# Contiguous operands for the gate-matrix matmuls of a hybrid decoder layer

## The chip, the cores and the metric

The kernel runs on one core of a Trainium2 chip. The metric is the device time of one execution in microseconds (us). Engines are TensorE (PE in the profile; PEld its weight loads), VectorE (DVE), ScalarE (ACT), GpSimd (POOL) and SyncE (SP). SP, ACT and POOL also issue DMAs.

## What is computed

One layer: RMSNorm, an input projection, differential attention and an mLSTM in parallel, an output projection, then PEER, a retrieval of single-neuron experts, and a gated embedding at the end. The change is in PEER. For each of 1024 tokens and 8 heads it finds 16 experts among 128 x 128 by two half keys, with softmax weights:

```python
eidx = jnp.take_along_axis(cidx, pos, axis=-1)      # i0 * 128 + i1
g = jax.nn.softmax(top_s, axis=-1)
a = jax.nn.gelu(jnp.einsum('td,thkd->thk', xb, expert_u[eidx]), approximate=False)
return jnp.einsum('thk,thkd->td', (g * a), expert_v[eidx])
```

## The kernel before

**Stages.** `front(0)` and `front(1)` do norms, projections, attention, mLSTM and the top-k of half the tokens each. `dense_up`, `dense_down` and `tail` follow. Three of the eight token tiles (NS = 3) take the experts by gathers (`sparse`: 384 gathers `ru` from expert_u, each multiplied on VectorE in line 808, and 384 `rv` from expert_v, accumulated into `ya` in line 826). The other five tiles (NDT = 5, 640 tokens, TD) are done densely: all 16384 experts are computed and weighted by a gate matrix that is zero where an expert was not chosen.

**The up stage** (`dense_up`) loops over 128 columns j. Each loads a table of 128 experts (`raw`, 512 KB, on SP's queue, three tiles), ScalarE rounds it to `thi` (line 845, two tiles), VectorE makes the rest `tlo` (line 846), and TensorE forms A: 24 matmuls of 384 token columns and 24 of 256, in the order (thi with the rounded and the rest of the tokens, then tlo). ScalarE applies GELU out of PSUM into `ga` (line 958, two pieces) and its queue stores it to `ga_s`. At each j, `pump` also lets 0.9 (the first 40 columns) or 1.45 pairs of gathers of `sparse` be emitted, at a lower priority than everything near (LAG = 800).

**The gate blocks** (`gate_blocks`) build the gate matrix, token by token: for a token t, the 128 x 128 matrix of gates is the product of two one-hot matrices over its 128 (head, k) pairs, the second weighted. The 128 pairs lie on the partitions. `it` holds, per partition, i0, i1, the weight rounded to 16 bits, and the rest of the weight, each for 128 tokens. Groups of 16 tokens are handled together: 40 groups in all. VectorE writes `o0` (i0 equals iota), `o1` (i1 equals iota), `w0` = o1 x weight and `w1` = o1 x rest, each 2048 fp16 elements laid out as [4, 128, 4]: the token b = 0 to 3 is innermost, so neighbours in memory are four tokens and `o0[:, a, :, b]`, the operand of one token, has a step of four elements. For each quarter a, eight matmuls (four tokens, w0 and w1, lines 898 and 899) fill one PSUM tile `pg` (three tiles), and ScalarE copies it to `st` (line 901; 512 elements, written with a step of GB = 32 elements). Each of o0, o1, w0 and w1 is one tile. After two groups `st` (32 tokens, 2 MB) is stored to `g_s` on SP's queue (line 904).

**Order.** The order on each engine is fixed when the program is built: a scheduler takes the instructions by their place in the program text and by when its model says that they are ready. Gate groups are emitted only after `late`, the top-k of the remaining tiles, is used up. From then on, after column j, the loop of line 965 emits groups until done x GSP >= (j - GST) x nb, with GSP = 105, GST = 14, and nb = 40 `yield`s of the generator. When `late` ends, the groups that are due by then come together. The sequence on VectorE that gathers and `tlo` share is held together by `anchor` and `behind`.

**The down stage** (`dense_down`) reads `g_s` and `ga_s` back, multiplies them, and accumulates with expert_v; `tail` ends the layer.

Of the kernel before, what the change touches and what calls it, by code (L numbers as in the profile page):

```python
# [11 lines left out]
F16 = mybir.dt.float16  # L12
I32 = mybir.dt.int32
U32 = mybir.dt.uint32
AF = mybir.ActivationFunctionType
OP = mybir.AluOpType
# [3 lines left out]
P = 128  # L20
# [19 lines left out]
NDT = S // P - NS  # L40
# [16 lines left out]
LATE = 1  # L57
HEAD = 200
WIDE = ("r1", "ro", "ry", "r2")
ACTW = 0  # L60
VB = 1
KORD = ("h", "r", "l")
GSP = 105
# [3 lines left out]
GB = 32  # L67
# [10 lines left out]
def layer(ctx, tc, x, xT, pT, gcols, grows, win, convw, convb, gbias, lams, wout, wq, subk,  # L78
# [3 lines left out]
    def pool(name, bufs=1, **k):  # L82
        if k.get("space") != bass.MemoryType.DRAM:
            k["reuse_waits"] = "tile"
        return tc.tile_pool(name=name, bufs=bufs, **k)

    v, sc, pe, gp, sy = nc.vector, nc.scalar, nc.tensor, nc.gpsimd, nc.sync
# [5 lines left out]
    def load_const(src, shape, name, pl_=const, dt=F32):  # L93
        t = pl_.tile(shape, dt, name=name)
        sy.dma_start(t, src)
        return t
# [752 lines left out]
    def table(dp, src, raw=None):  # L849
        raw = dp.tile([P, 1024], F32, name="raw", bufs=3) if raw is None else raw  # L850
        hi = dp.tile([P, 1024], F32R, name="thi", bufs=2)
        lo = dp.tile([P, 1024], F32R, name="tlo", bufs=2)
        split(raw, src, hi, lo)
        return hi, lo

    def gate_blocks(gp_, pT_, pG):
        ioe = gp_.tile([P, P, 4], F16, name="ioe")
        iof = load_const(iota_d[None, :].to_broadcast([P, P]), [P, P], "iof", gp_)
        v.tensor_copy(ioe, iof[:, :, None].to_broadcast([P, P, 4]))
        sh = [P, 4, P, 4]  # L860
        io = ioe[:, None].to_broadcast(sh)
        for n, tl in enumerate(DORD):
            part, i = divmod(tl, NT)
            fl = gp_.tile([P, 3, P], F32, name="fl", bufs=1)
            v.tensor_copy(fl[:, 0], sel_i[part][0][:, i, :])
            v.tensor_copy(fl[:, 1], sel_i[part][1][:, i, :])
            v.tensor_scalar(fl[:, 2], gsm[part][:, i, :], WSC, None, op0=OP.mult)
            pt = pT_.tile([P, 3, P], F32, name="pt")
            for c in range(3):
                pe.transpose(pt[:, c, :], fl[:, c, :], ident)  # L870
            it = gp_.tile([P, 4, P], F16, name="it", bufs=2)
            v.tensor_copy(it[:, 0:3], pt)
            v.tensor_tensor(it[:, 3], pt[:, 2], it[:, 2], op=OP.subtract)
            if ACTW:
                wlo = fl[:, 2]
                v.tensor_tensor(wlo, pt[:, 2], it[:, 2], op=OP.subtract)
            for hb in range(P // GB):
                st = gp_.tile([P, P, GB], F32, name="st", bufs=64 // GB)
                for sb in range(GB // 16):
                    tb = slice(hb * GB + sb * 16, hb * GB + sb * 16 + 16)  # L880
                    iv = [it[:, c, tb].rearrange("p (a b) -> p a b", b=4)[:, :, None, :].to_broadcast(sh)
                          for c in range(4)]
                    o0 = gp_.tile(sh, F16, name="o0", bufs=1)
                    o1 = gp_.tile(sh, F16, name="o1", bufs=1)
                    w0 = gp_.tile(sh, F16, name="w0", bufs=1)
                    w1 = gp_.tile(sh, F16, name="w1", bufs=1)
                    v.tensor_tensor(o0, iv[0], io, op=OP.is_equal)
                    v.tensor_tensor(o1, iv[1], io, op=OP.is_equal)
                    v.tensor_tensor(w0, o1, iv[2], op=OP.mult)
                    if ACTW < 4:  # L890
                        v.tensor_tensor(w1[:, :4 - ACTW], o1[:, :4 - ACTW], iv[3][:, :4 - ACTW], op=OP.mult)
                    for a in range(4):
                        for b in range(4) if a >= 4 - ACTW else ():
                            t_ = hb * GB + sb * 16 + a * 4 + b
                            sc.activation(w1[:, a, :, b], o1[:, a, :, b], AF.Copy, scale=wlo[:, t_:t_ + 1])
                        pg = pG.tile([P, 4, P], F32, name="pg")
                        for b in range(4):
                            pe.matmul(pg[:, b, :], o0[:, a, :, b], w0[:, a, :, b], start=True, stop=False)  # L898
                            pe.matmul(pg[:, b, :], o0[:, a, :, b], w1[:, a, :, b], start=False, stop=True)  # L899
                        t_ = sb * 16 + a * 4  # L900
                        sc.activation(st[:, :, t_:t_ + 4].rearrange("p j t -> p t j"), pg, AF.Copy,
                                      scale=1.0 / WSC)
                    yield True
                sy.dma_start(g_s[n * (P // GB) + hb], st)

    def chain(*gens):
        for g in gens:
            yield from g()

    def dense_up(ptk):  # L910
        qh, ql = fcs["q"]
        chunks = [(qh, ql, 0, CH1)]
        with ExitStack() as c1:
            dp = c1.enter_context(pool("dp"))
            gp_ = c1.enter_context(pool("gp"))
            pA = c1.enter_context(pool("pA", bufs=2, space=PSUM))
            pT_ = c1.enter_context(pool("pT_", space=PSUM))
            pG = c1.enter_context(pool("pG", bufs=3, space=PSUM))
            raw = dp.tile([P, 1024], F32, name="raw", bufs=3)
            gas = [dp.tile([P, TD], F32, name="ga", bufs=3)]  # L920
            if NX:
                xh = dp.tile([P, DC, NX], F32R, name="xh")
                xl = dp.tile([P, DC, NX], F32R, name="xl")
                chunks.append((xh, xl, CH1, TD - CH1))

            head = [table(dp, ut[0], raw)]

            def extra_columns():
                for n, tl in enumerate(DORD[CH1 // P:]):
                    h2 = gp_.tile([P, D], F32, name="st", bufs=64 // GB)  # L930
                    sy.dma_start(h2, h2_s[tl])
                    for q in range(2):
                        pt = pT_.tile([P, 4, P], F32, name="pt")
                        for j in range(4):
                            pe.transpose(pt[:, j, :], h2[:, (4 * q + j) * P:(4 * q + j + 1) * P], ident)
                        dst = (slice(None), slice(4 * q, 4 * q + 4), slice(n * P, (n + 1) * P))
                        sc.activation(xh[dst], pt, AF.Copy)  # L937
                        v.tensor_sub(xl[dst], pt, xh[dst].bitcast(F32))

            late = chain(lambda: topk2(0, ptk, [2]), lambda: topk2(1, ptk, [0, 2]))  # L940
            gates = gate_blocks(gp_, pT_, pG)
            nb, done = 8 * NDT, 0
            for j in range(P):
                pump(UP_RATE[0 if j < UP_RATE[2] else 1])
                hi, lo = head.pop() if head else table(dp, ut[j])
                ga = gas.pop() if gas else dp.tile([P, TD], F32, name="ga", bufs=3)
                ps = pA.tile([P, 2, 512], F32, name="A")
                terms = [[(ps[:, n, :w], hi[:, dc * P:(dc + 1) * P], lo[:, dc * P:(dc + 1) * P], rh[:, dc, :w],
                           rl[:, dc, :w], dc == 0, dc == DC - 1) for dc in range(DC)]
                         for n, (rh, rl, o, w) in enumerate(chunks)]  # L950
                if j == 0:
                    mm3s(terms[0], ("hr", "l"))
                    extra_columns()
                    mm3s(sum(terms[1:], []), ("hr", "l"))
                else:
                    mm3s(sum(terms, []), ("hr", "l"))
                for n, (rh, rl, o, w) in enumerate(chunks):
                    sc.activation(ga[:, o:o + w], ps[:, n, :w], AF.Gelu)
                sc.dma_start(ga_s[j], ga)
                if late is not None:  # L960
                    for _ in range(LATE):
                        if late is not None and next(late, None) is None:
                            late = None
                    continue
                while done < nb and done * GSP < (j - GST) * nb:
                    next(gates, None)
                    done += 1
            for _ in gates:
                pass
# [292 lines left out]
```

## Time and profile before

| | us |
|---|---|
| median of 3 runs (3181.86 to 3189.38) | 3186.96 |
| profiled execution | 3192.56 |
| span of its instructions | 3190.8 |
| TensorE busy in the span | 2954.2 (93%) |
| VectorE busy | 2512.5 (79%) |
| ScalarE busy | 1159.0 (36%) |
| the up stage, first A matmul to last `ga` | 1031 to 2115 |
| gate matmuls, first to last | 1362 to 2044 |

A row of a group of instructions reads: line, engine, operation, output and inputs, shape, count, then busy us and mean ns of one, then the idle time of the engine before them and what ended it. A matmul's record begins when it starts streaming and ends when its result is out, so matmuls overlap: how far apart two start tells what one costs in a stream.

### The profile page before, as it was taken

How to read it: one execution, taken by the hardware profiler on the slowest of the kernel's cores; microseconds unless marked ns; L12 is line 12 of the kernel's file. 1: busy time of each engine (PE TensorE's matmuls, PEld its weight loads, DVE VectorE, ACT ScalarE, POOL GpSimd, SP SyncE). 2: the span in 40 equal slices, each digit the busy share in tenths (PEclk: the TensorE clock that was granted, in tenths of full speed). 3: DMA queues.
4: the chain of work that ended last, by engine and by line, in shares of the span. 5: the costliest groups of instructions: out<-in, count | busy, mean ns of one | idle time of the engine just before them, and what ended most of it. 6: DMA issues, size and time to landing. Idle time of an engine off the chain costs nothing.

```text
span 3190.8 us, 44623 instructions
## 1 busy us (share of the span) xinstructions
PE 2954.2 (93%) x16367; PEld 2599.5 (81%) x16367; DVE 2512.5 (79%) x5321; ACT 1159.0 (36%) x1992; POOL 1021.9 (32%) x786
## 2 busy tenths in 40 slices
PE   7997889887777999999899999988999999999987
PEld 6786767776666899999899999977878888887866
DVE  5564689887679998777877768667888888888886
ACT  5664335555322222264333343322212222222233
POOL 0000000343312433403554435443434444342331
PEclk9998989998798999999999999989999999999998
DMA  5333433676745877858998989999999999998773
GB/s 165 96 106 110 144 119 96 211 230 203 255 178 178 311 276 264 302 217 308 344 355 333 335 300 342 345 368 337 333 334 339 338 338 333 332 317 277 265 236 126
DMA packets 317147, 829.52 MB, mean 260 GB/s; under 512 B 26240, under 2 KB 115200, under 8 KB 314368
## 3 DMA queue, kind: packets, MB, share of 16 engines
q0 software_dynamic: 112608, 410.04, 36.3%
q1 hardware_dynamic: 185888, 374.68, 33.9%
q10 hardware_dynamic: 18432, 41.95, 3.5%
q8 instruction: 128, 2.10, 0.3%
q14 instruction: 91, 0.75, 0.1%
HBM read 715.95 MB, written 102.24 MB: 256 GB/s over the span
## 4 chain that ended last, share of the span: by engine, by line
PE 29%; DMA 7%; DVE 7%; issue 7%; POOL 1%; ACT 1%; DVEq 0%; SPq 0%; POOLq 0%; ACTq 0%
PE A L145 13%; PE keep L145 6%; DMA raw<-in_vr 3%; DMA rv<-in_ev,eidx 2%; PE Y L137 2%; PE Y L136 2%; PE Y L138 2%; DVE ya L826 2%; PE pg L898 1%; PE pg L899 1%; DMA ru<-in_eu,eidx 1%; DVE tlo L846 1%; DVE ru L808 1%; DVE aq L1024 1%; DVE yac L1045 1%
## 5 line engine op out<-in xcount | busy, mean ns | idle before, releaser
L792 POOL DMA_INDIRECT ru<-in_eu,eidx x384 | 499.5, 1301 | 1165.4 <-DVE ru L808 857.0
L792 POOL DMA_INDIRECT rv<-in_ev,eidx x384 | 514.4, 1340 | 465.7 <-DVE ya L826 321.1
L826 DVE SCALAR_TENSOR_TENSOR ya<-rv,cf,ya 128x1024 f32<-128x1024 f32 x384 | 492.5, 1283 | 44.6 <-DMA rv<-in_ev,eidx 33.6
L846 DVE TENSOR_TENSOR tlo<-raw,thi 128x1024 fp32r<-128x1024 f32 x256 | 312.5, 1221 | 263.5 <-ACT thi L845 143.6
L845 ACT ACTIVATE thi<-raw 128x1024 fp32r<-128x1024 f32 x256 | 267.8, 1057 | 685.4 <-PE A L145 353.5
L808 DVE SCALAR_TENSOR_TENSOR ru<-ru,sh 128x1024 f32<-128x1024 f32 x384 | 467.9, 1219 | 27.0 <-DMA ru<-in_eu,eidx 24.4
L145 PE MATMUL A<-ahi,thi 128*128 128x384 f32 x1024 | 349.5, 341 | 14.1 <-ACT thi L845 13.8
L145 PE MATMUL A<-alo,thi 128*128 128x384 f32 x1024 | 346.9, 339 | 0.2 <-issue 0.2
L145 PE MATMUL mm<-ahi,whi 128*128 128x512 f32 (+1 forms) x752 | 300.0, 403 | 21.2 <-ACT ahi L236 12.8
L145 PE MATMUL mm<-alo,whi 128*128 128x512 f32 (+1 forms) x752 | 286.6, 394 | 7.1 <-DVE alo L237 7.1
L136 PE MATMUL Y<-thi,ph 128*128 128x512 f32 x640 | 250.8, 392 | 7.5 <-ACT thi L845 5.6
L137 PE MATMUL Y<-tlo,ph 128*128 128x512 f32 x640 | 250.1, 391 | 2.1 <-DVE tlo L846 2.1
L145 PE MATMUL A<-xh,thi 128*128 128x256 f32 x1024 | 251.3, 283 | 0.7 <-ACT xh L937 0.7
L145 PE MATMUL A<-xl,thi 128*128 128x256 f32 x1024 | 251.3, 283 | 0.0
L138 PE MATMUL Y<-thi,pl 128*128 128x512 f32 x640 | 249.3, 390 | 0.0
L1025 ACT ACTIVATE ph<-aq 128x640 fp32r<-128x640 f32 x128 | 87.4, 728 | 338.1 <-PE Y L137 332.9
L145 PEld LDWEIGHTS A<-ahi,thi 128*128 128x128 f32 x1024 | 195.5, 191 | 14.4 <-ACT thi L845 14.0
L145 PE MATMUL A<-ahi,tlo 128*128 128x384 f32 x1024 | 201.1, 336 | 0.3 <-DVE tlo L846 0.3
L145 PE MATMUL mm<-ahi,wlo 128*128 128x512 f32 (+1 forms) x752 | 193.1, 388 | 5.5 <-DVE wlo L196 5.5
L145 PEld LDWEIGHTS A<-xh,thi 128*128 128x128 f32 x1024 | 195.4, 191 | 0.9 <-ACT xh L937 0.9
L145 PEld LDWEIGHTS A<-alo,thi 128*128 128x128 f32 x1024 | 195.3, 191 | 0.5 <-issue 0.5
L145 PEld LDWEIGHTS A<-xl,thi 128*128 128x128 f32 x1024 | 195.4, 191 | 0.0
(462 smaller groups left out, 6121.4 us busy)
## 6 DMA issues: line engine op xcount, KB each, us to landing
raw<-in_ut SPq DMA_DIRECT2D x128, 512.0 KB
raw<-in_vr SPq DMA_DIRECT2D x128, 512.0 KB
ga_s<-ga ACTq DMA_DIRECT2D x128, 320.0 KB
g_s<-st SPq DMA_DIRECT2D x20, 2048.0 KB
gq<-g_s SPq DMA_DIRECT2D x32, 1280.0 KB
aq<-ga_s SPq DMA_DIRECT2D x32, 1280.0 KB
wraw<-in_win SPq DMA_DIRECT2D x58, 512.0 KB
wraw<-in_wq SPq DMA_DIRECT2D x32, 512.0 KB
```

Source lines behind the costliest of these rows:

```text
L136: pe.matmul(o, lh, rh, start=start, stop=False)
L137: pe.matmul(o, lh, rl, start=False, stop=False)
L138: pe.matmul(o, ll, rh, start=False, stop=stop)
L145: pe.matmul(o, ll if p == "l" else lh, rl if p == "r" else rh, start=start and p == "h", stop=stop and n == last and p == names[-1])
L792: gp.indirect_dma_start(out=b, out_offset=None, in_=table, in_offset=bass.IndirectOffsetOnAxis(ap=eidx[part][:, i, k:k + 1], axis=0))
L808: behind(v.scalar_tensor_tensor(b, b, 1.0, st["h", tl], op0=OP.mult, op1=OP.mult, accum_out=st["d", n][:, j:j + 1]))
L826: op = v.scalar_tensor_tensor(ya, b, st["c", n][:, j:j + 1], ya, op0=OP.mult, op1=OP.add)
L845: sc.activation(hi, raw, AF.Copy)
L846: anchor(v.tensor_sub(lo, raw, hi.bitcast(F32)))
L898: pe.matmul(pg[:, b, :], o0[:, a, :, b], w0[:, a, :, b], start=True, stop=False)
L899: pe.matmul(pg[:, b, :], o0[:, a, :, b], w1[:, a, :, b], start=False, stop=True)
L1025: sc.activation(ph, av, AF.Copy)
```

## The change

`o0` is now laid out [16, 128], each token's 128 elements contiguous, and written by one compare whose first input repeats each token's i0 over 128 places and whose second is the iota (every fourth element of the tile `ioe`, which holds each number four times). `o1` and `w0` keep the interleaved layout; `o1` is overwritten in place by o1 x rest, and `w1` is gone. For each half group (a = 0 and a = 2) ScalarE copies the two weighted matrices, eight tokens each, from the interleaved order into a new tile `wc`, one tile in size of w1, contiguous for each token: two copies of 1024 elements. The matmuls read `o0` and `wc`. The compare for o0 moves behind the other three VectorE operations. The generator yields after each half group, and nb is 80 in place of 40. The setting ACTW, which was 0, and the code under it are removed.

```diff
-                    o0 = gp_.tile(sh, F16, name="o0", bufs=1)
+                    o0 = gp_.tile([P, 16, P], F16, name="o0", bufs=1)
                     o1 = gp_.tile(sh, F16, name="o1", bufs=1)
                     w0 = gp_.tile(sh, F16, name="w0", bufs=1)
-                    w1 = gp_.tile(sh, F16, name="w1", bufs=1)
-                    v.tensor_tensor(o0, iv[0], io, op=OP.is_equal)
                     v.tensor_tensor(o1, iv[1], io, op=OP.is_equal)
                     v.tensor_tensor(w0, o1, iv[2], op=OP.mult)
-                    if ACTW < 4:
-                        v.tensor_tensor(w1[:, :4 - ACTW], o1[:, :4 - ACTW], iv[3][:, :4 - ACTW], op=OP.mult)
+                    v.tensor_tensor(o1, o1, iv[3], op=OP.mult)
+                    v.tensor_tensor(o0, it[:, 0, tb][:, :, None].to_broadcast([P, 16, P]),
+                                    ioe[:, None, :, 0].to_broadcast([P, 16, P]), op=OP.is_equal)
                     for a in range(4):
+                        if a % 2 == 0:
+                            wc = gp_.tile([P, 2, 2, 4, P], F16, name="wc", bufs=1)
+                            for c, w in enumerate((w0, o1)):
+                                sc.activation(wc[:, c], w[:, a:a + 2].rearrange("p a j b -> p a b j"), AF.Copy)
                         pg = pG.tile([P, 4, P], F32, name="pg")
                         for b in range(4):
-                            pe.matmul(pg[:, b, :], o0[:, a, :, b], w0[:, a, :, b], start=True, stop=False)
-                            pe.matmul(pg[:, b, :], o0[:, a, :, b], w1[:, a, :, b], start=False, stop=True)
+                            for c in range(2):
+                                pe.matmul(pg[:, b, :], o0[:, 4 * a + b, :], wc[:, c, a % 2, b, :], start=c == 0,
+                                          stop=c == 1)
...
-                    yield True
+                        if a % 2:
+                            yield True
...
-            nb, done = 8 * NDT, 0
+            nb, done = 16 * NDT, 0
```

## Rows read from the trace of the kernel before

**Rows 1.** The span in 40 slices: busy tenths of TensorE and of DMA
```profile
PE   7997889887777999999899999988999999999987
...
DMA  5333433676745877858998989999999999998773
```

**Rows 2.** Windows: length, busy us of PE, PEld, DVE, ACT, POOL, clock, DMA, GB/s
```profile
1100.00:1200.00 100.00, 100.00 (x684) 100.00 (x683) 98.22 (x311) 29.87 (x47) 41.92 (x32) 1.00 0.79 290
1356.00:1500.00 144.00, 143.99 (x1078) 138.62 (x1077) 118.22 (x122) 83.55 (x100) 29.19 (x21) 1.00 0.67 246
1500.00:2116.00 616.00, 602.68 (x4249) 598.56 (x4247) 461.34 (x519) 228.35 (x320) 303.80 (x224) 0.99 0.91 339
1356.00:2116.00 760.00, 746.67 (x5325) 737.17 (x5323) 579.56 (x641) 311.90 (x419) 332.99 (x245) 0.99 0.87 321
2116.00:3035.00 919.00, 886.10 (x3844) 725.84 (x3844) 761.19 (x972) 221.00 (x275) 357.56 (x273) 0.98 0.93 325
```

**Rows 3.** Windows of the gate tile pg alone: length, PE, ACT, clock, DMA, GB/s
```profile
1356.00:1500.00 144.00, 65.87 (x512) 63.66 (x64) 1.00 0.67 246
```

**Rows 4.** Groups of 16-bit matmuls and weight loads; L415 loads by minimum/median/maximum ns
```profile
L898 PE MATMUL pg<-w,o 128*128 128x128 f16 x640 | 152.5, 297 | 11.4 <-DVE w L889 11.4
...
L899 PEld LDWEIGHTS <-o 128*128 128x128 f16 x640 | 75.1, 117 | 3.8 <-issue 2.6
...
L415 PE MATMUL S<-maskneg,identb 128*128 128x128 bf16 x64 | 14.8, 232 | 0.0
...
L415 PEld LDWEIGHTS <-identb x64: 95/96/152, 53.3 to 784.8; 128*128 128x128 bf16 x64
```

**Rows 5.** Timeline of single matmuls: start us, duration us, engine, line
```profile
1409.55 0.29 PE L899 MATMUL pg<-w,o 128*128 128x128 f16 x1
...
1410.13 0.30 PE L898 MATMUL pg<-w,o 128*128 128x128 f16 x1
...
1414.19 0.28 PE L145 MATMUL A<-xh,thi 128*128 128x256 f32 x1
...
1415.02 0.28 PE L145 MATMUL A<-xl,thi 128*128 128x256 f32 x1
...
1413.15 0.33 PE L145 MATMUL A<-ahi,thi 128*128 128x384 f32 x1
...
1414.02 0.33 PE L145 MATMUL A<-alo,thi 128*128 128x384 f32 x1
...
699.84 0.39 PE L145 MATMUL mm<-alo,whi 128*128 128x512 f32 x1
...
701.44 0.39 PE L145 MATMUL mm<-ahi,whi 128*128 128x512 f32 x1
```

**Rows 6.** Groups of VectorE, shapes kept apart
```profile
L887 DVE TENSOR_TENSOR o<-it,ioe 128x2048 f16<-128x2048 f16 x40 | 49.0, 1224 | 51.7 <-PE pg L899 51.7
...
L846 DVE TENSOR_TENSOR tlo<-raw,thi 128x1024 fp32r<-128x1024 f32 x256 | 312.5, 1221 | 263.5 <-ACT thi L845 143.6 <-issue 117.5
...
L1141 DVE TENSOR_TENSOR yac<-gt,yac 128x512 f32<-128x512 f32 x10 | 6.6, 682 | 0.0
...
L749 DVE COPY i<-dl 128x256 bf16<-128x256 bf16 x4 | 1.1, 278 | 0.0
...
L751 DVE COPY bb<-pos 128x256 bf16<-128x256 bf16 x4 | 0.9, 218 | 0.0
```

**Rows 7.** Groups of ScalarE between 1031 and 2116 us
```profile
L901 ACT ACTIVATE st<-pg 128x512 f32<-128x512 f32 x160 | 159.5, 1141 | 37.5 <-PE pg L899 35.5 <-issue 1.9
L845 ACT ACTIVATE thi<-raw 128x1024 fp32r<-128x1024 f32 x128 | 135.8, 1061 | 429.1 <-PE A L145 353.5 <-DVE ya L826 39.3 <-remote 10.3
L958 ACT ACTIVATE ga<-A 128x384 f32<-128x384 f32 (+1 forms) x256 | 98.4, 437 | 171.1 <-PE A L145 152.0 <-issue 19.0
...
L937 ACT ACTIVATE xh<-pt 128x512 fp32r<-128x512 f32 x4 | 2.4, 598 | 13.0 <-PE pt L935 13.0
```

**Rows 8.** Waits from 1356 to 2046 us: total us, times, longest us
```profile
ACT thi L845 <- PE A L145: 199.9, 60, 4.7
...
DVE o L887 <- PE pg L899: 51.7, 34, 2.4
...
PE pg L898 <- DVE w L889: 11.4, 1, 11.4
```

More of the change, by code (lines that the diff above doesn't have):

```diff
@@ L59 @@
 WIDE = ("r1", "ro", "ry", "r2")
-ACTW = 0
 VB = 1
@@ L873, in gate_blocks @@
             v.tensor_tensor(it[:, 3], pt[:, 2], it[:, 2], op=OP.subtract)
-            if ACTW:
-                wlo = fl[:, 2]
-                v.tensor_tensor(wlo, pt[:, 2], it[:, 2], op=OP.subtract)
             for hb in range(P // GB):
@@ L882, in gate_blocks @@
                           for c in range(4)]
-                    o0 = gp_.tile(sh, F16, name="o0", bufs=1)
+                    o0 = gp_.tile([P, 16, P], F16, name="o0", bufs=1)
                     o1 = gp_.tile(sh, F16, name="o1", bufs=1)
                     w0 = gp_.tile(sh, F16, name="w0", bufs=1)
-                    w1 = gp_.tile(sh, F16, name="w1", bufs=1)
-                    v.tensor_tensor(o0, iv[0], io, op=OP.is_equal)
                     v.tensor_tensor(o1, iv[1], io, op=OP.is_equal)
                     v.tensor_tensor(w0, o1, iv[2], op=OP.mult)
-                    if ACTW < 4:
-                        v.tensor_tensor(w1[:, :4 - ACTW], o1[:, :4 - ACTW], iv[3][:, :4 - ACTW], op=OP.mult)
+                    v.tensor_tensor(o1, o1, iv[3], op=OP.mult)
+                    v.tensor_tensor(o0, it[:, 0, tb][:, :, None].to_broadcast([P, 16, P]),
+                                    ioe[:, None, :, 0].to_broadcast([P, 16, P]), op=OP.is_equal)
                     for a in range(4):
-                        for b in range(4) if a >= 4 - ACTW else ():
-                            t_ = hb * GB + sb * 16 + a * 4 + b
-                            sc.activation(w1[:, a, :, b], o1[:, a, :, b], AF.Copy, scale=wlo[:, t_:t_ + 1])
+                        if a % 2 == 0:
+                            wc = gp_.tile([P, 2, 2, 4, P], F16, name="wc", bufs=1)
+                            for c, w in enumerate((w0, o1)):
+                                sc.activation(wc[:, c], w[:, a:a + 2].rearrange("p a j b -> p a b j"), AF.Copy)
                         pg = pG.tile([P, 4, P], F32, name="pg")
                         for b in range(4):
-                            pe.matmul(pg[:, b, :], o0[:, a, :, b], w0[:, a, :, b], start=True, stop=False)
-                            pe.matmul(pg[:, b, :], o0[:, a, :, b], w1[:, a, :, b], start=False, stop=True)
+                            for c in range(2):
+                                pe.matmul(pg[:, b, :], o0[:, 4 * a + b, :], wc[:, c, a % 2, b, :], start=c == 0,
+                                          stop=c == 1)
                         t_ = sb * 16 + a * 4
```

## Prediction

> **What bounds the kernel now.** I read the page's slices first, then the windows of the stage that the change touches, then its groups of instructions, then single matmuls in the timeline. The slices [rows 1] show TensorE nearly full from the first third of the span to the end, with the DMA engines nearly full too from the middle on. The gate blocks run inside the up stage, between 1356 and 2116 us. There TensorE is busy 746.67 of 760 us, VectorE 579.56, ScalarE 311.90, at clock 0.99 [rows 2]: TensorE sets the end of this stage. The stage falls in two. In the first 144 us, 512 of the 1280 gate matmuls run, 16 of the 40 groups of 16 tokens, and DMA is at 0.67; in the other 616 us the gates are thin and DMA stands at 0.91 with 339 GB/s [rows 2, 3]. Waits of TensorE for the gates' operands are one of 11.4 us in the whole stage [rows 8]. So what the change takes from TensorE is gained, unless something else fills the 760 us: DMA moves 321 GB/s over them [rows 2], 244 MB, and is the next in line.
>
> **What a gate matmul costs.** It has 128 columns and yet one starts every 116 ns: 0.58 us for five steps from 1409.55 to 1410.13 [rows 5]. Matmuls with contiguous operands start every 119 ns at 256 columns (0.83 us for seven), 174 ns at 384 (0.87 for five) and 229 ns at 512 (1.60 for seven) [rows 5]. That is about 55 ns for 128 columns, and a line through them gives 64 ns at 128. The gate matmul thus pays for 256 columns. Its record says the same: 297 ns, while the one matmul of this kernel with 16-bit contiguous operands of 128 columns lasts 232 ns, 65 ns less; and its weight load lasts 117 ns against 96 [rows 4]. What sets the gates apart is that both operands are read with a step of four elements, 8 bytes. I take 64 ns after the change. The ends are 55 ns (only the slope) and 117 ns (the step is not the cause). In between lies 96 ns, if the contiguous weight load of that length paces the pair.
>
> [...]
>
> **The change part by part.** TensorE: 1280 x (117 - 64) ns = 68 us less (ends 79 and 0, at 96 ns 27 us). The stage would last 692 us if TensorE went on setting it.
>
> VectorE: the first operand is still one compare of 2048 elements, but its inputs are now a value repeated with step 0 and an iota read with step 4, and no longer four neighbours at a time. Now it takes 1224 ns, as long as 1024 fp32 elements (1221): two 16-bit elements where fp32 has one [rows 6]. Where a 16-bit copy in this trace reads a repeated value, 256 elements cost 278 ns instead of 218 [rows 6], so packing does suffer. I take one element at a time: 512 fp32 elements cost 682 ns, 1024 cost 1221, 1.053 ns each, so 2048 cost 1221 + 1078 = 2299 ns. 40 x 1.08 = 43 us more, and nothing at the low end; below nothing is excluded, since the pattern loses neighbours and wins none. The multiplication that wrote w1 now writes o1 and costs what it did. VectorE goes to 623 us, 87% of the 714 us forecast below. Earlier in the stage it was busy 98.22 of 100 us with TensorE full [rows 2], so I cost this at nothing; if the cover is gone it is 43 us.
>
> ScalarE: per 16 tokens four copies are added, each of 1024 16-bit elements, read with step 4, written contiguous; 160 in all. No row shows a 16-bit source read so. The nearest is the copy of 1024 fp32 elements, 1061 ns. The low end is half of that, 0.53 us, if 16-bit goes two at a time. The high end comes from the copy out of PSUM that writes with a step of 32 elements: 1141 ns for 512, where a contiguous one takes 598 [rows 7], 1.06 ns more per element, so 1.06 + 1.09 = 2.15 us. I take 1.06, since the new copy writes contiguous and reads with a short step: 160 x 1.06 = 170 us (85 to 344). ScalarE goes from 312 to 482 us of the stage. Nothing on the path, if it is spread: it waits 199.9 us for A matmuls to free the thi tile [rows 8].
>
> The new waits: a copy waits for w0 and o1, and, wc being one tile, for the 16 matmuls that read the last one. Behind a waiting copy on ScalarE stand thi (the next column's table), the GELU ga and its DMA on the same queue, and the copies out of PSUM. TensorE waits for thi, VectorE for thi before tlo, and tlo stands before the sparse part's gathers. In return VectorE no longer waits for the gate matmuls before it rewrites w0 and o1, only for the copies; o0 alone still waits for TensorE (these waits cost VectorE 51.7 us [rows 8]). After the first 144 us a half group comes every 1.3 columns (80 over the 105 of GSP), over 9 us at 24 x (119 + 174) ns = 7.0 us of A matmuls per column, and its two copies take 2.1: hidden. In the first 144 us, 16 groups come at once. On ScalarE one costs 4 x 1.06 + 4 x 1.14 = 8.8 us, where now a group passes every 9 us (144/16): the gates then proceed at ScalarE's pace, and TensorE fills with A matmuls of later columns, which need from ScalarE only 1.06 us for thi and 2 x 0.44 for ga [rows 7] per 7 us. I cost it at nothing; what it costs without that cover is the last rival's price. That the generator hands over half groups, twice as often, changes only where in the order they stand. SBUF is the same: w1 leaves, wc of equal size comes. The store of st to g_s stays in SP's queue ahead of raw loads of later columns; it waits for the last copy out of PSUM as now, and three raw tiles are ahead of need: no cost while the groups do not fall behind.
>
> DMA: no byte changes, but the same 244 MB come in less time. The first part shortens by 512 x 53 ns = 27 us to 117. The other 339 GB/s x 616 us = 209 MB would take 560 us at full share (339/0.91 = 373 GB/s), and then TensorE's 692 us for the stage hold; with no more throughput than now they take 616, the stage 117 + 616 = 733. These are 68 and 27 us of gain. I take the middle, 350 GB/s or 0.94: 597 + 117 = 714 us, a gain of 46. The down stage runs at 0.93 [rows 2], so a share like that holds for long, but with TensorE full only in part (886 of 919 us). The stages behind start when A ends and nothing of theirs changes, so the gain reaches the end.
>
> **Sum.** The profiled execution took 3192.56 us, its span 3190.8. 3192.6 - 46 = 3147. The median of the runs before is 5.6 us under that execution: 3141 us.
>
> **Rivals.** DMA doesn't bind: gathers move into the first 144 us, where DMA has a third free, and TensorE keeps its 68 us: 3119 us. For it, the low share at the beginning; against it, VectorE does those gathers and is fullest there.
>
> The weight load paces the pair at 96 ns: 27 us, 3160. For it, loads and matmuls alternate one to one; against it, a gate load lasts as long as its slot, which would be so for either operand.
>
> The operands' step is not the cause, or the change doesn't reach it: nothing saved, VectorE's and ScalarE's additions hidden, 3187. [...] For it, the 256-column matmul has the same 117 ns; against it the two record lengths.
>
> ScalarE sets the pace where 16 groups come at once, and the A matmuls do not fill in, since thi stands behind gate copies in ScalarE's order. A group then lasts 8.8 us plus half a column's thi and ga (1.0), 9.8, where TensorE needs 32 x 64 ns and half a column of A, 3.5 us, together 5.5. 16 x 4.3 = 69 us lost eats the whole 68. Above 1.06 us per copy the kernel is slower: at 1.5 us a group lasts 11.5 and 16 x 6.0 = 96 us are lost, 28 net: 3215. For it, ScalarE's fixed order and the one wc tile; against it, in the trace ScalarE's waits are for TensorE, not the reverse.
>
> **Chances.** Forecast (3119 to 3160) 0.52, no bound by DMA 0.13, load-paced 0.10, nothing saved 0.09, ScalarE's pace 0.16. A measurement of this kernel tells about 0.2%, 6.4 us, from no change. Faster: 0.52 + 0.13 + 0.10 = 0.75. Nothing saved is mostly the same, 0.07, with 0.02 to slower: 0.18. The range takes in the 55 ns end (79 us, 3108) and goes up to 3184, where the pair would save next to nothing; it leaves out ScalarE's pace and little else.
>
> **What would show it.** In the profile after: gate matmuls 64 ns apart and near 232 ns long, with loads near 96; the o0 compare at 2.3 us; 160 copies at 1.06; TensorE as full as before from 1356 on and DMA at 0.94 behind the burst; A's last matmul 46 us earlier and the down stage as long as now. It is wrong if gate matmuls stay at 117 ns, if copies pass 1.5 us, or if TensorE shows new waits for wc or thi.

## The result and the profile after

The changed kernel takes 3140.26 us (median of four runs, 3135.79 to 3143.68) beside 3185.61 (3181.86 to 3189.38; four runs, one more than in the table above) before: a ratio of 0.9854 [0.9836, 0.9872], its 95% interval in brackets, 45 us less. 3141 was forecast. The profiled execution took 3138.16 us, its span 3136.4, so the two profiles lie 54.4 us apart; that of before was 7 us above its median, that of after 2 under.

The slices of the page after, busy tenths, as in [rows 1]:

```profile
PE   7997889987789799999999999979999999999987
...
ACT  5664326554422232257787656422222222222133
...
DMA  5333423566664788889998999999999999998763
```

TensorE is nearly as full as before, with one dip to 7 where the up stage ends; ScalarE has its new work from the eighteenth slice on. Where the 54.4 us lie is read from the first and the last A matmul (count, minimum/median/maximum ns, first and last start). First two rows of before, then two of after:

```profile
L145 PE MATMUL A<-ahi,thi x1024: 334/334/687, 1031.4 to 2109.6; 128*128 128x384 f32 x171
L145 PE MATMUL A<-xh,tlo x1024: 275/281/560, 1050.4 to 2114.1; 128*128 128x256 f32 x171
```

```profile
L144 PE MATMUL A<-ahi,thi x1024: 331/335/690, 1039.1 to 2056.9; 128*128 128x384 f32 x171
L144 PE MATMUL A<-xh,tlo x1024: 277/282/365, 1058.1 to 2061.3; 128*128 128x256 f32 x171
```

From first to last A matmul it is 2114.1 - 1031.4 = 1082.7 us before and 2061.3 - 1039.1 = 1022.2 after: 60.5 us less. The stage began 7.7 us later, with the order of the instructions up to there unchanged (over all kernels of this study it began between 1028 and 1039). The down stage took 911.3 in place of 914.7 us, the tail 158.0 in place of 156.4. 60.5 - 7.7 + 3.4 - 1.6 = 54.6. The whole gain thus lies in the up stage, and I compare the kernels below by these 1082.7 and 1022.2 us beside their times. Such a length comes from one execution and is not exact: two kernels below, whose gate matmuls and whose times are as before, have 1074.1 and 1074.2 us.

The windows of the stage after, columns as in [rows 2], and one of pg alone, columns as in [rows 3]:

```profile
1365.00:1500.00 135.00, 126.23 (x1027) 121.05 (x1026) 125.58 (x128) 107.81 (x126) 62.76 (x43) 1.00 0.89 325
1500.00:1710.00 210.00, 196.72 (x1594) 188.29 (x1594) 195.74 (x196) 166.49 (x195) 95.80 (x69) 1.00 0.91 340
1710.00:2005.00 295.00, 293.75 (x2276) 291.69 (x2276) 253.57 (x265) 184.54 (x232) 151.98 (x111) 1.00 0.95 357
1365.00:2062.00 697.00, 673.32 (x5281) 657.45 (x5279) 613.30 (x632) 471.68 (x575) 339.59 (x244) 1.00 0.93 347
```

```profile
1364.00:1708.00 344.00, 62.63 (x816) 106.76 (x102) 1.00 0.90 334
```

The gates that come together now take 344 us, not 144: 816 of the 1280 gate matmuls, 25.5 groups, one every 13.5 us. TensorE idles in that part (135.00 - 126.23 and 210.00 - 196.72, 22 us) and hardly behind it (1.25 us of 295). VectorE is at 93% there (125.58 of 135, 195.74 of 210), ScalarE at 80% and 79%.

The groups of the gates between 1031 and 2070 us (busy us, mean ns of one, idle before them by what ended it), which answer to [rows 4], [rows 6] and [rows 7]:

```profile
L895 PE MATMUL pg<-wc,o 128*128 128x128 f16 x1280 | 94.4, 220 | 23.3 <-ACT wc L891 21.1 <-ACT st L898 0.9 <-issue 0.7
L895 PEld LDWEIGHTS <-o 128*128 128x128 f16 x1280 | 75.7, 98 | 38.9 <-issue 33.1 <-DVE o L885 0.3 <-PE A L144 0.2
L891 ACT ACTIVATE wc<-w 128x1024 f16<-128x1024 f16 x80 | 92.1, 1151 | 18.8 <-DVE w L883 17.6 <-ACT ga L956 1.2
L891 ACT ACTIVATE wc<-o 128x1024 f16<-128x1024 f16 x80 | 91.7, 1146 | 13.2 <-DVE o L884 11.5 <-ACT ga L956 1.6
L885 DVE TENSOR_TENSOR o<-it,ioe 128x2048 f16<-128x2048 f16 x40 | 91.5, 2288 | 3.2 <-PE pg L895 2.6 <-PE A L144 0.2
```

And the waits between 1364 and 2062 us (who waits, for whom: sum, count, longest), as in [rows 8]:

```profile
ACT thi L844 <- PE A L144: 93.9, 54, 4.6
...
DVE o L882 <- ACT wc L891: 22.2, 23, 2.1
PE pg L895 <- ACT wc L891: 21.1, 24, 1.0
ACT wc L891 <- DVE w L883: 17.6, 21, 1.6
DVE o L885 <- PE pg L895: 2.6, 6, 1.0
...
DVE ya L825 <- DMA rv<-in_ev,eidx: 1.8, 2, 0.9
DVE ru L807 <- DMA ru<-in_eu,eidx: 1.3, 3, 0.8
```

The matmul's record has gone from 297 to 220 ns, its weight load from 117 to 98. VectorE's 51.7 us of waits for gate matmuls have become 2.6, and 22.2 for the copies. New is a row of TensorE: 24 waits for `wc`, up to 1.0 us each, 21.1 us in all. One of them in the timeline, first of TensorE and then of ScalarE (start, duration, line; in brackets the idle time before it):

```profile
1450.52 0.34 PE L144 MATMUL A<-ahi,thi 128*128 128x384 f32 x1
1451.82 0.27 PE L895 MATMUL pg<-wc,o 128*128 128x128 f16 x2 [0.96 <-ACT wc L891]
...
1452.86 0.96 PE L895 MATMUL pg<-wc,o 128*128 128x128 f16 x14
1453.63 0.42 PE L144 MATMUL A<-ahi,thi 128*128 128x384 f32 x1
```

```profile
1450.63 1.14 ACT L891 ACTIVATE wc<-w 128x1024 f16<-128x1024 f16 x1
1451.64 1.14 ACT L891 ACTIVATE wc<-o 128x1024 f16<-128x1024 f16 x1
```

The first copy ends at 1450.63 + 1.14 = 1451.77 us; TensorE, which had A matmuls to do, stands from 1450.86 to 1451.82. The gates' place in its order comes before those A matmuls. The 14 matmuls behind the second copy show the new price: (0.96 - 0.22)/13 = 57 ns apart.

Two figures are worked out from the start times of all matmuls in the stage. Neighbouring gate matmuls start 118 ns apart before and 56 after (medians): 1280 x 62 = 79 us less. And where a gate matmul follows an A matmul, the time between their starts beyond the usual 174 or 119 ns sums to 12.0 us before (11.6 of them in one step, the wait of 11.4 in [rows 8]) and to 30.7 after, over 50 steps: 19 us more. I call this second sum the excess. 79 - 19 = 60, the measured 60.5. The clock has no part in the 118 and 56 ns: the granted clock is 1.00 in the burst before [rows 2] and in the one after, and an A matmul of 384 columns takes 174 ns in both. The sum holds for this pair of executions; between kernels with the same matmuls the length differs by 8 us, as said above. So the question for the experiments is what makes TensorE wait in front of the gates, and which operand's order was worth the 79 us.

### The profile page after: what moved, and what is told of

Same layout as the page of the kernel before. It is cut to its first block, busy times and chain, and to the rows that moved or that the text cites. A ratio compares the mean times of both kernels' runs of the same rounds, so it can differ in the third digit from the quotient of the medians.

```text
span 3136.4 us, 44806 instructions
## 1 busy us (share of the span) xinstructions
PE 2890.3 (92%) x16367; PEld 2531.0 (81%) x16367; DVE 2552.5 (81%) x5321; ACT 1320.9 (42%) x2152; POOL 1027.0 (33%) x786
## 4 chain that ended last, share of the span: by engine, by line
PE 62%; DVE 12%; issue 10%; DMA 9%; ACT 5%; POOL 2%; SPq 0%; DVEq 0%; ACTq 0%; POOLq 0%
PE A L144 24%; PE mm L144 11%; PE keep L144 7%; DMA raw<-in_vr 3%; PE Y L136 3%; PE Y L135 3%; PE Y L137 3%; DMA rv<-in_ev,eidx 3%; PE S L144 2%; PE pg L895 2%; DVE ya L825 2%; DVE ru L807 1%; ACT st L898 1%; DMA ru<-in_eu,eidx 1%; ACT wc L891 1%
## 5 line engine op out<-in xcount | busy, mean ns | idle before, releaser
L807 DVE SCALAR_TENSOR_TENSOR ru<-ru,sh 128x1024 f32<-128x1024 f32 x384 | 468.0, 1219 | 23.7 <-DMA ru<-in_eu,eidx 23.7
```

What stands on the lines that cost most here:

```text
L807: behind(v.scalar_tensor_tensor(b, b, 1.0, st["h", tl], op0=OP.mult, op1=OP.mult, accum_out=st["d", n][:, j:j + 1]))
```

## The experiments

Three theories of the 19 us: **S**, the single tile `wc` ties copies and matmuls to each other; **D**, DMA, which the prediction named: TensorE is held back because tables or gathers come late; **O**, the order fixed in advance puts gate matmuls close behind copies that end later than was allowed for. Each ratio below is to runs of the kernel before on the same chip, whose medians were 3191.55 to 3192.64 us there, so ratios and not times compare with the 0.9854 above.

**A second tile wc.** `it` and `ga` give up a buffer and the iota moves into the place of `fl`, so that it fits.

```diff
-wc = gp_.tile([P, 2, 2, 4, P], F16, name="wc", bufs=1)
+wc = gp_.tile([P, 2, 2, 4, P], F16, name="wc", bufs=2)
```

> The changed kernel (3140 us) with two wc tiles instead of one; to make room in SBUF, ga has two tiles instead of three, it one instead of two, and the iota is loaded into the place of fl. Theory S (TensorE's gain is partly given back because the copies of a half group wait for the matmuls that read the one wc tile, and TensorE then waits for the copies): the 24 waits of about 1 us for wc in the changed kernel's up stage (21 us) mostly go, and the time falls by 10 to 24 us, to 3116 to 3130. Theory D (DMA takes it back): the stage stays as long, 3134 to 3146.

3141.74 us, ratio 0.9841 [0.9824, 0.9858]; first to last A matmul 1030.2 us. Two rows of its waits in the stage:

```profile
PEld L896 <- DVE o L886: 16.4, 3, 10.4
...
PE pg L896 <- ACT wc L892: 13.9, 7, 12.4
```

The many waits of about 1 us for `wc` are gone (7 in place of 24), but one of 12.4 us came, and one of 10.4 for VectorE's o0. The time that S forecast did not come back: the kernel is no faster. This alone does not refute S, since `ga` and `it` have fewer buffers here and the order is another one; the run doesn't say what a second tile would bring in the same order.

**Gates spread over the stage.** They start later and follow at a steady pace.

```diff
-GSP = 105
-GST = 14
+GSP = 75
+GST = 44
```

> The changed kernel with its gate groups spread: GST = 44 and GSP = 75, so that no groups are overdue when the gates begin, one half group per column. Theory S: where groups come one at a time, ScalarE keeps up, TensorE's waits for wc (21 us) vanish, 3116 to 3130. Theory D: the DMA load per time is the same in the mean, 3134 to 3146.

3135.37 us, 0.982 [0.9799, 0.984]; 1028.3 us from first to last A matmul. The row of TensorE's waits:

```profile
PE pg L895 <- ACT wc L891: 26.9, 26, 4.7
```

The waits stay, and the excess is 35.0 us. The time is in D's range, and its interval overlaps that of the changed kernel run again (0.9844 [0.9821, 0.9867], below), so a gain is not shown. That 26 groups come back to back is thus not by itself their cause.

**Half the bytes of the tables.** Each column loads 512 of its 1024 values per partition and reads them twice; the other half of each table is left out.

```diff
-raw = dp.tile([P, 1024], F32, name="raw", bufs=3)
+raw = dp.tile([P, 512], F32, name="raw", bufs=3)
+sy.dma_start(raw, src[:, 0:512])
+rb = raw[:, None, :].to_broadcast([P, 2, 512])
```

> The changed kernel with half the table loaded in the up stage: each column's raw holds 512 of its 1024 elements per partition, and ScalarE and VectorE read them twice (so the dense part computes with wrong tables; the work of every engine is the same). 33.6 MB fewer, about a tenth of what DMA moves in the stage. Theory D: with the DMA engines relieved the stage ends 20 us or more earlier, 3120 or below. Theory S: nothing waits for DMA there, 3134 to 3146.

3137.69 us, 0.9842 [0.9819, 0.9864]; 1021.0 us from first to last A matmul. Its window of the stage and its row of waits:

```profile
1360.00:2055.00 695.00, 671.49 (x5272) 656.14 (x5271) 610.91 (x629) 470.67 (x573) 339.25 (x244) 1.00 0.87 318
```

```profile
PE pg L899 <- ACT wc L895: 23.1, 27, 1.0
```

DMA has fallen from 0.93 and 347 GB/s to 0.87 and 318, and neither the time nor the waits have moved. D falls: the stage isn't held by DMA.

**Only the moving operand contiguous.** o0 goes back to the interleaved layout and its old compare; the copies into `wc` stay.

```diff
-o0 = gp_.tile([P, 16, P], F16, name="o0", bufs=1)
+o0 = gp_.tile(sh, F16, name="o0", bufs=1)
-pe.matmul(pg[:, b, :], o0[:, 4 * a + b, :], wc[:, c, a % 2, b, :], start=c == 0,
+pe.matmul(pg[:, b, :], o0[:, a, :, b], wc[:, c, a % 2, b, :], start=c == 0,
```

> The changed kernel with o0 interleaved as before (and its compare as before); only the moving operand wc is contiguous. Theory: the moving operand's step of 8 bytes is what cost the second half of each gate matmul's 117 ns, so the matmuls start 56 to 64 ns apart here too; the weight loads stay at 117 ns each by their records, beside the matmuls. Rival (the weight load with that step sets the pace): about 117 ns apart, time 3186. If it is shared, something between, such as 96 ns.

A single execution: 3133.52 us beside 3191.88 of the kernel before. Its groups:

```profile
L894 PE MATMUL pg<-wc,o 128*128 128x128 f16 x1280 | 95.6, 221 | 26.2 <-ACT wc L890 25.7
L894 PEld LDWEIGHTS <-o 128*128 128x128 f16 x1280 | 80.6, 115 | 41.2 <-issue 32.9 <-DVE o L885 2.4 <-DVE tlo L845 0.3
```

The matmuls start 56 ns apart and last 221 ns, as with both contiguous, though the loads are back at 115 ns.

**Only the stationary operand contiguous.** o0 as in the change; w1 is back and the matmuls read the interleaved w0 and w1; no copies.

```diff
+w1 = gp_.tile(sh, F16, name="w1", bufs=1)
-v.tensor_tensor(o1, o1, iv[3], op=OP.mult)
+v.tensor_tensor(w1, o1, iv[3], op=OP.mult)
-wc[:, c, a % 2, b, :]
+(w0, w1)[c][:, a, :, b]
```

> The changed kernel with o0 contiguous, but the moving operands w0 and w1 interleaved as before and read directly, so without the copies on ScalarE. Theory (the moving operand's step is the cause): the gate matmuls start 117 ns apart, time 3180 to 3192. Rival (the weight load's step is): 56 to 64 ns apart, and as nothing waits for copies the time is at or below that of the changed kernel, 3105 to 3140.

3191.37 us beside 3191.55, 1.0007 [0.9993, 1.0021]. Its groups:

```profile
L892 PE MATMUL pg<-w,o 128*128 128x128 f16 x1280 | 158.8, 294 | 10.7 <-DVE w L884 6.8 <-DVE o L886 3.9
L892 PEld LDWEIGHTS <-o 128*128 128x128 f16 x1280 | 139.8, 114 | 16.2 <-DVE w L884 7.4 <-DVE o L886 4.4 <-issue 1.4
```

116 ns apart, records of 294, 1074.2 us from first to last A matmul: nothing is gained. The two runs together show that all of the 79 us comes from the moving operand. The load lasts 114 ns here though its operand is contiguous (98 in the changed kernel, whose matmuls start 56 ns apart), so its record also follows the pace of the matmuls. This kernel also has the 2.3 us compare, and no loss: its 43 us on VectorE are hidden here, beside slow matmuls.

**A contiguous iota** for the o0 compare, of which the value repeated with step 0 stays.

```diff
+ioc = gp_.tile([P, P], F16, name="ioc")
+v.tensor_copy(ioc, iof)
-ioe[:, None, :, 0].to_broadcast([P, 16, P])
+ioc[:, None, :].to_broadcast([P, 16, P])
```

> The changed kernel with the second input of the o0 compare contiguous (an iota of its own in fp16) while the first still repeats one value with step 0. If the repeated value keeps the compare at one element at a time, it stays at 2.29 us; if the iota's step of four did, it falls to 1.22 us. Total within 6 us of the changed kernel either way, if VectorE is hidden.

**Pairs.** Beside the contiguous iota, the values of i0 are doubled in a small tile `i2`, so that both inputs have two neighbours in memory; the fp32 iota moves into the place of `fl`, as with the second `wc`.

```diff
-v.tensor_tensor(o0, it[:, 0, tb][:, :, None].to_broadcast([P, 16, P]),
-                ioe[:, None, :, 0].to_broadcast([P, 16, P]), op=OP.is_equal)
+v.tensor_tensor(o0.rearrange("p t (j b) -> p t j b", b=2),
+                i2[:, tb][:, :, None, :].to_broadcast([P, 16, 64, 2]),
+                ioc.rearrange("p (j b) -> p j b", b=2)[:, None].to_broadcast([P, 16, 64, 2]),
+                op=OP.is_equal)
```

> The changed kernel with the o0 compare's first input doubled beforehand, so that it reads pairs of neighbours (i0 twice) against a contiguous iota: the innermost run is two elements with step 1. Expected: the compare takes 1.22 us instead of 2.29, 43 us less on VectorE. Theory H (VectorE's longer compare is hidden): time within 6 us of the changed kernel, 3134 to 3146. Rival V (VectorE, 88% busy in the stage, holds up the copies and so TensorE): 3115 to 3130.

The group of the compare in the first and then in the second:

```profile
L887 DVE TENSOR_TENSOR o<-it,ioc 128x2048 f16<-128x2048 f16 x40 | 91.4, 2286 | 3.6 <-PE pg L897 3.3 <-PE A L144 0.2
```

```profile
L890 DVE TENSOR_TENSOR o<-i,ioc 128x2048 f16<-128x2048 f16 x40 | 48.8, 1219 | 1.5 <-PE pg L902 0.9 <-PE A L144 0.5
```

The iota's step doesn't matter (2286 ns contiguous, 2288 with the step; a single execution, 3142.26 us); the repeated value does, and pairs restore 1219 ns. The kernel with pairs takes 3150.49 us, 0.988 [0.986, 0.9899]: 43 us less on VectorE made it no faster, and some 10 us slower. TensorE still waits 27.2 us for `wc`, in 30 waits, so it is not the longer compare alone that makes it wait. From first to last A matmul it took 1037.0 us. The kernel with the contiguous iota alone took 1037.7 us there with the long compare, so the longer stage does not come from the pairs. Its order is another one, and I could not settle what in it costs more.

**Half groups handed over in the kernel before.**

```diff
-                    yield True
+                        if a % 2:
+                            yield True
-nb, done = 8 * NDT, 0
+nb, done = 16 * NDT, 0
```

> The kernel before with the finer hand-over alone: the generator yields after each half group and nb is 80; operands, compares and matmuls as before. If the finer steps have no part in the gain: 3180 to 3192. If they have, 3150 to 3180.

3192.2 us, 0.9994 [0.9976, 1.0013]; 1074.1 us from first to last A matmul. The finer steps have no part in the gain, as costed.

**Matmuls one step behind their copies.** The generator now yields between the copies and the matmuls that read them, so that what else is due is placed between.

```diff
                             for c, w in enumerate((w0, o1)):
                                 sc.activation(wc[:, c], w[:, a:a + 2].rearrange("p a j b -> p a b j"), AF.Copy)
+                            yield True
...
-                        if a % 2:
-                            yield True
...
-nb, done = 16 * NDT, 0
+nb, done = 16 * NDT + 1, 0
```

> The changed kernel with the hand-over of the generator moved between the copies and the matmuls: the 16 matmuls of a half group stand in the program one step behind their copies. Theory O (TensorE waits, 30 us in all before gate matmuls in the changed kernel's up stage, because the fixed order puts the matmuls right behind copies that end later on the chip): where half groups come 1.3 columns apart, the waits vanish; where they come back to back they stay. The changed kernel's waits lie mostly in the back-to-back part, so 5 to 15 us faster than the changed kernel: 3125 to 3135. Rival (the waits are TensorE's share of a loop of ScalarE and VectorE that takes so long in any order): 3134 to 3146.

3140.67 us, 0.9843 [0.982, 0.9867]; 1023.9 us, excess 31.0. Its row of waits:

```profile
PE pg L896 <- ACT wc L891: 23.8, 26, 3.5
```

By itself it changes nothing: O's forecast missed and the time is in the rival's range. My reading is that where groups are emitted together, the next step follows at once and no column comes between.

**The same, with the gates spread** (GSP 75, GST 44).

> The same hand-over, and the half groups spread one per column (GSP = 75, GST = 44). Theory O: copies end a column ahead of their matmuls, the waits before gate matmuls (35 us with the spread alone) fall below 10, and the time to 3105 to 3118. Rival (the loop of ScalarE and VectorE takes so long): waits of 25 us or more stay and the time is that of the spread alone, 3129 to 3141.

3122.85 us, 0.9782 [0.9758, 0.9806]; from first to last A matmul 1007.1 us, excess 12.2. Its window of the stage, its row of waits, and its A matmuls:

```profile
1373.00:2038.00 665.00, 652.00 (x5169) 643.04 (x5168) 599.59 (x619) 465.65 (x566) 330.69 (x237) 1.00 0.94 355
```

```profile
PE pg L896 <- ACT wc L891: 7.1, 9, 1.8
```

```profile
L144 PE MATMUL A<-ahi,thi x1024: 333/334/689, 1031.1 to 2033.7; 128*128 128x384 f32 x171
L144 PE MATMUL A<-xh,tlo x1024: 278/281/363, 1050.1 to 2038.2; 128*128 128x256 f32 x171
```

With a column's matmuls between the copies and their readers, the excess falls from 30.7 to 12.2 us, with the same copies of 1.16 us, the same single tile and the same bytes; DMA carries more (355 GB/s). Between one gate matmul and the next, which the excess leaves out, the gaps beyond 56 ns sum to 6.3 us here and to 0.6 in the changed kernel, so TensorE's waits at the gates fell by some 13 us and not by the whole 18.5. The start and end times show the order itself: in the changed kernel the first gate matmul of a half group starts within 0.2 us of the end of its first copy in 42 of 80 half groups, and in the median 0.06 us after it; here in 15 of 80, and 4.1 us after it. This speaks for O, and against S as the sole cause: the waits are made by where the order puts the gate matmuls. The time is between the two forecast ranges, a few us above O's.

**The changed kernel again**, on the chip of the last two.

> The changed kernel once more, beside the two others on the same chip: 3134 to 3146. A second profile shows which waits belong to the order (the waits of about 1 us before gate matmuls, 30 us in all) and which to the one execution.

3143.39 us, 0.9844 [0.9821, 0.9867]; excess 31.2.

```profile
PE pg L895 <- ACT wc L891: 21.5, 25, 1.0
```

The same waits in another execution (21.1 us in 24 at first). Against it the spread and lagged kernel gains 3143.39 - 3122.85 = 20.5 us, of which 1024.4 - 1007.1 = 17.3 between the first and the last A matmul.

**What both findings make together:** the lag, the spreading, and o0 interleaved with its old compare.

> The kernel with the matmuls one step behind their copies and the half groups spread (3123 us), but o0 interleaved as before, with the old compare of 1.22 us. If the contiguous stationary operand has no part in TensorE's time and VectorE is hidden: 3117 to 3129, gate matmuls 56 ns apart. If VectorE's 43 us count in this order: 3100 to 3117. If the slower weight load counts: over 3129.

3117.82 us, 0.9767 [0.9743, 0.9791], the fastest; 1009.1 us from first to last A matmul. Its row of waits:

```profile
PE pg L895 <- ACT wc L890: 2.9, 5, 1.0
```

The gate matmuls start 56 ns apart beside loads of 115 ns, and the compare takes 1217 ns. The time is at the lower edge of the first range. From the kernel before it (0.9782) it can't be told apart, though VectorE has 43 us less to do. A contiguous o0 isn't needed.

## Why the prediction was right or wrong

**The bound: right.** TensorE set the end of the stage, and what left it was gained, less new waits.

**The matmul: right in kind, 8 ns too dear.** Taken were 64 ns, with 55 as the low end from the slope between 256 and 512 columns; measured were 56. The intercept of the line through the fp32 matmuls doesn't hold for this one. The saving is 79 us, not 68. The load doesn't pace the pair: beside a contiguous moving operand it lasts 98 ns contiguous and 115 interleaved, and both times the matmuls start 56 ns apart. That a gate load lasted as long as its slot [rows 4] was no sign of either. The "why" was half wrong too: of the two operands read with a step, only the moving one cost anything, 118 ns a matmul against 56.

**VectorE: right.** 2299 ns were forecast for the compare and 2288 measured; the two kernels with contiguous and with doubled inputs show that the repeated value is the reason. It was at 613.30 of 697 us, 88% for 87 forecast. That its 43 us are hidden is seen twice: added without the other half of the change they give 1.0007, and taken away from the spread kernel 0.9767 beside 0.9782. The second pair has intervals of 0.0024 to either side, some 8 us, so it leaves room for a few us of the 43 to count.

**ScalarE: size slightly off, the place right, the price not nothing.** A copy takes 1.15 us, not 1.06. The load was taken from idle time: ScalarE's waits for A matmuls went from 199.9 [rows 8] to 93.9 us. But "I cost it at nothing" failed: TensorE waits 21.1 us for `wc`, and new waits for `wc` are one of the signs by which the prediction said that it would be wrong. The prediction's last rival had the right place, copies that end after TensorE comes to their readers where groups follow on each other, but not its mechanism or its size: ScalarE is at 80% there and not full, and A matmuls do fill in (TensorE is busy 126.23 of 135.00 and 196.72 of 210.00 us). The groups came every 13.5 us, not every 9. What the runs speak for instead is an order that puts the reader right behind the copy. My reason against it, that in the trace ScalarE waits for TensorE and not the reverse, is a statement on a trace without such a reader.

**DMA: wrong.** 22 us of the gain were to be taken back by 350 GB/s. The stage carried 347, near the forecast, but VectorE waited only 1.8 and 1.3 us for gathers, with half the table bytes nothing changed, and the spread kernel carried 355. A share near 0.93 was read as a ceiling, without a row of anyone waiting for transfers. The sum's other premise failed too: the 144 us in which the gates come together did not shrink to 117 but became 344, with 25.5 groups in place of 16.

**The sum: right by two errors.** 68 - 22 = 46 us were forecast; 79 - 19 = 60 were found in the stage, 54.4 between the profiled executions and 45 between the medians. Against the two kernels with the old matmul price and 1074 us the stage gained 52. The loss had about the right size by luck: it was put in the wrong place, and the saving was 11 us too small. The place matters: a loss to DMA would have had to stay, while the kernel with the lag and the spread is 20.5 us faster than the changed one.

**Open** stays why the orders with a second `wc` and with pairs cost as much as they removed. Both kernels free or shorten something and are then laid out anew; I have no run in which the order stays and only the duration changes. That the copies end later than the order allowed for is inferred from where TensorE waits; no run shows the times that the order was built with.

## What to carry to other kernels

Look at the step of the moving operand first: here, where neighbours in the stream weren't neighbours in memory, a gate matmul cost 118 ns in place of 56, copies of 1.15 us on ScalarE, which had idle time, paid for themselves, and the stationary operand could be left as it was (0.9767 beside 0.9782). A hidden copy must be ahead of its reader in the order, not only fit into idle time; place the readers a step later, and spread them, so that there is other work in between: both together took TensorE's waits for `wc` from 21.1 to 7.1 us, with the lag alone they were 23.8 and with the spreading alone 26.9. Before a high DMA share is put into a sum as a limit, see whether anyone waits for a transfer: at the 0.93 here VectorE waited 1.8 and 1.3 us for gathers.

## What the runs showed of the hardware

A 128-column 16-bit matmul whose moving operand had a step of 8 bytes cost 116 to 118 ns in a stream, as much as 256 contiguous columns of fp32 (119); contiguous it cost 56. The same step in the stationary operand, beside a contiguous moving one, lengthened the load from 98 to 115 ns and left the matmuls 56 ns apart. A VectorE compare of 2048 16-bit elements took 2286 to 2288 ns with step 0 innermost in one input, and 1219 where both inputs had pairs. ScalarE read 1024 16-bit elements with a step of 8 bytes in 1.15 us, and copied 1024 contiguous fp32 elements in 1.06.
